# Normalising softmax probabilities on VectorE instead of GpSimd in a three-layer transformer kernel

## The chip, the cores and the metric

The program runs on one core of one Trainium2 chip. The metric is device time of one launch in microseconds. Times below are medians of executions on the chip; the profile is one execution of the same program, recorded instruction by instruction.

## What is computed

Two transformer blocks stand one after the other, on 512 tokens of width 1024, in float32. The first has two layers, the second one. Each layer is a mixer with several kinds of attention and a feed-forward part. The five softmax attentions are what the change touches:

```python
# layer 0: fox (8 heads, causal, forget gates) and chk (8 heads, chunks with a bias)
p = softmax(where(mask, q @ k.T * scale + bias, -inf));  o = p @ v
# layer 1: MLA (8 heads, chunk-causal); beside it 8 stick-breaking heads without a softmax
# layer 2: diff (4 heads)      a = softmax(s0) - lam * softmax(s1);  o = a @ v
#          NSA (8 heads)       o = g0 * o_cmp + g1 * (softmax(s_sel) @ v_sel) + g2 * (softmax(s_win) @ v_win)
```

All heads work on 512 queries by 512 keys. The rest are matrix products with the weights (projections, feed-forward), RMS norms, rotary embeddings and gates.

## The kernel before

**Tiling.** Activations lie transposed, 128 features by 512 tokens a tile. Weights stream from HBM in blocks of 128x1024 (`wblock`, L585). TensorE multiplies in a reduced form of float32, so every operand is kept as a high and a low part: ScalarE copies a block to its high part `wh`, VectorE subtracts to get the low part `wl`, and each product is three matmuls (`gemm`, L598). VectorE and ScalarE split activations in the same way.

**A softmax head.** `soft_head` (L820) does the four blocks of 128 queries of a head; block i has n = 128(i+1) keys. For each block `softmax` (L745) has two or three score matmuls into PSUM `pss`; then VectorE adds the mask and takes the row minimum in one custom instruction and reads its accumulator, ScalarE does the exponential with its row sum, VectorE the reciprocal of the sum, and GpSimd multiplies the block by the reciprocal (and in NSA by a gate column `gt`) in place. Then `turn` (L761) transposes on TensorE into PSUM `psp` and splits into `pt`, high part on ScalarE and low part on VectorE; `av` (L775) multiplies by the values into PSUM `pso`; `fold` (L782) adds the halves, `T<-pso,T` on VectorE, once a head. In diff heads every second block goes out unnormalised (`gate == "raw"`). The probability blocks are tiles `x`, their row statistics `sm`.

**The order of the work.** Nothing is issued directly. A recorder (L250) takes all instructions with what they read and write, and `schedule` (L391) places them: a list scheduler with a cost for each instruction (L322) and a latency between engines. On each engine it picks, of what is ready by its own clock, the instruction with the lowest priority number; attention comes first, and projections that are needed later (written under `later`) fill the gaps. In chk these fillers are the next heads' projections and half of the output projection; in NSA they are the products `ya`, `mg0` and `mg1` with their gates. Each engine then runs its queue in that order, and waits where a result isn't there yet. The cost of an instruction depends on its engine, so that a moved instruction shifts the order on all engines. All instructions are issued from L372, and so all rows of the profile have that line; the names of the tiles tell them apart. PSUM `psg` is what projections write.

```python
        if op.name == "tensor_scalar":            # GpSimd
            return 160 + 0.836 * n + 83 * k
        ...
            if op.name in ("memset", "tensor_copy") or (op.name == "tensor_scalar" and not psum):
                return 67 + 0.53 * n + 58 * k     # VectorE
```

Of the kernel before, what the change touches and what calls it, by code (L numbers as in the profile page):

```python
# [15 lines left out]
ALU = mybir.AluOpType  # L16
# [486 lines left out]
class Net:  # L503
# [241 lines left out]
    def softmax(self, i, passes, bias, gate=None):  # L745

        nc = self.nc
        n = 128 * (i + 1)
        s = self.scores(i, passes)
        p = self.tl("x", [128, 512])  # L750
        m = self.small(4)
        nc.vector.tensor_tensor_reduce(p[:, :n], s[:, :n], bias(i), scale=1.0, scalar=3e38,
                                       op0=ALU.add, op1=ALU.min, accum_out=m[:, 0:1])
        nc.scalar.activation(p[:, :n], p[:, :n], AF.Exp, scale=-1.0, bias=m[:, 0:1], accum_out=m[:, 1:2])
        nc.vector.reciprocal(m[:, 2:3], m[:, 1:2])
        if gate == "raw":
            return p, m[:, 2:3]
        nc.gpsimd.tensor_scalar(p[:, :n], p[:, :n], m[:, 2:3], 1.0 if gate is None else gate(i), ALU.mult, ALU.mult)
        return p

    def turn(self, ps_list):  # L761
# [1006 lines left out]
```

## Time and profile before

| | |
|---|---|
| median of three runs | 2076.8 us (2076.6 to 2078.18) |
| the profiled execution's own time | 2076.13 us |
| its span, first to last instruction | 2074.1 us |
| TensorE busy (weight loads beside it) | 97% (81%) |
| VectorE busy | 55% |
| ScalarE busy | 43% |
| GpSimd busy | 19% |
| mean granted TensorE clock | 0.993 of full speed |

The shares are means over the whole span. Attention takes some stretches of it, and in those VectorE and ScalarE are much busier than their means say; feed-forward stretches are TensorE's alone.

### The profile page before, as it was taken

How to read it: one execution, taken by the hardware profiler on the slowest of the kernel's cores; microseconds unless marked ns; L12 is line 12 of the kernel's file. 1: busy time of each engine (PE TensorE's matmuls, PEld its weight loads, DVE VectorE, ACT ScalarE, POOL GpSimd, SP SyncE). 2: the span in 40 equal slices, each digit the busy share in tenths (PEclk: the TensorE clock that was granted, in tenths of full speed). 3: DMA queues.
4: the chain of work that ended last, by engine and by line, in shares of the span. 5: the costliest groups of instructions: out<-in, count | busy, mean ns of one | idle time of the engine just before them, and what ended most of it. 6: DMA issues, size and time to landing. Idle time of an engine off the chain costs nothing. (4 is left out here: it accounts for less than half of the span.)

```text
span 2074.1 us, 27228 instructions
## 1 busy us (share of the span) xinstructions
PE 2017.1 (97%) x9958; PEld 1683.7 (81%) x9958; DVE 1131.8 (55%) x2033; ACT 895.1 (43%) x1621; POOL 396.5 (19%) x524
## 2 busy tenths in 40 slices
PE   8999999999999999999999999989999999999998
PEld 7888878888888877778888888867788888888887
DVE  5667853434445576774434344766786644333334
ACT  5556542322335555653323243543685543222224
POOL 2343210000022463220000014211340221011013
PEclk9999999999999999999999999999999999999999
DMA  6445623333344315632333334473213222223232
GB/s 199 129 129 154 198 83 100 94 99 97 97 139 127 102 62 131 180 115 92 102 93 101 94 122 135 122 182 116 71 42 112 92 101 92 101 93 102 91 102 82
DMA packets 80293, 231.98 MB, mean 112 GB/s; under 512 B 11424, under 2 KB 15392, under 8 KB 80160
## 3 DMA queue, kind: packets, MB, share of 16 engines
q1 hardware_dynamic: 80160, 230.25, 36.8%
q8 instruction: 78, 1.28, 0.3%
q14 instruction: 55, 0.45, 0.1%
HBM read 183.04 MB, written 10.49 MB: 93 GB/s over the span
## 5 line engine op out<-in xcount | busy, mean ns | idle before, releaser
L372 PE MATMUL psg<-h,wh 128*128 128x512 f32 x2688 | 848.4, 393 | 0.9 <-ACT h L372 0.6
L372 ACT ACTIVATE wh<-wr 128x1024 fp32r<-128x1024 f32 (+3 forms) x313 | 326.3, 1042 | 846.0 <-PE psg L372 672.9
L372 PEld LDWEIGHTS psg<-h,wh 128*128 128x128 f32 x2688 | 503.3, 189 | 102.0 <-ACT h L372 1.5
L372 PE MATMUL psg<-h,wl 128*128 128x512 f32 x1344 | 528.9, 393 | 1.2 <-DVE wl L372 1.0
L372 DVE TENSOR_TENSOR wl<-wr,wh 128x1024 fp32r<-128x1024 f32 (+3 forms) x313 | 384.7, 1229 | 59.9 <-ACT wh L372 58.7
L372 PEld LDWEIGHTS psg<-h,wl 128*128 128x128 f32 x1344 | 253.6, 189 | 53.9 <-DVE wl L372 3.1
L372 PE MATMUL psg<-KK,wh 128*128 128x512 f32 (+1 forms) x788 | 237.8, 383 | 0.4 <-DVE V L372 0.2
L372 DVE TENSOR_TENSOR x<-psg,x 128x512 f32<-128x512 f32 (+1 forms) x120 | 78.2, 654 | 281.8 <-PE psg L372 281.7
L372 POOL TENSOR_TENSOR acc<-acc,T 128x512 f32<-128x512 f32 (+1 forms) x50 | 72.9, 1457 | 775.7 <-issue 627.3
L372 PE MATMUL psg<-V,wh 128*128 128x512 f32 (+1 forms) x672 | 205.7, 387 | 1.1 <-DVE G L372 1.1
L372 PEld LDWEIGHTS psg<-KK,wh 128*128 128x128 f32 x788 | 146.3, 188 | 29.5 <-ACT o L372 0.6
L372 PE MATMUL psg<-KK,wl 128*128 128x512 f32 (+1 forms) x394 | 150.8, 383 | 0.0
L372 PEld LDWEIGHTS psg<-V,wh 128*128 128x128 f32 x672 | 125.6, 188 | 27.3 <-ACT wh L372 1.2
L372 DVE SCALAR_TENSOR_TENSOR T<-psg,rbc 128x512 f32<-128x512 f32 x64 | 44.2, 691 | 167.2 <-PE psg L372 166.8
L372 ACT ACTIVATE x<-x,sm 128x128 f32<-128x128 f32 (+1 forms) x192 | 106.6, 558 | 54.7 <-DVE sm L372 53.9
L372 PE MATMUL psg<-V,wl 128*128 128x512 f32 (+1 forms) x336 | 129.9, 387 | 0.0
L372 PE MATMUL psg<-o,wh 128*128 128x512 f32 x384 | 126.2, 397 | 0.8 <-ACT wh L372 0.5
L372 PE MATMUL psg<-wh,h 128*128 128x256 f32 (+2 forms) x560 | 114.5, 292 | 6.6 <-ACT wh L372 6.6
L372 PE MATMUL pso<-pt,V 128*128 128x128 f32 (+3 forms) x432 | 108.8, 340 | 3.4 <-ACT pt L372 1.9
L372 POOL TENSOR_SCALAR x<-x,sm 128x128 f32<-128x128 f32 (+1 forms) x112 | 65.9, 594 | 174.6 <-DVE sm L372 122.8
L372 PEld LDWEIGHTS psg<-wh,h 128*128 128x128 f32 x560 | 92.4, 194 | 8.4 <-ACT wh L372 6.6
L372 POOL TENSOR_TENSOR T<-T,rbc 128x512 f32<-128x512 f32 x22 | 39.2, 1782 | 280.5 <-ACT T L372 280.5
(263 smaller groups left out, 2667.6 us busy)
## 6 DMA issues: line engine op xcount, KB each, us to landing
wr<-in_w_dram SPq DMA_DIRECT2D x302, 512.0 KB, 3.5
KK<-AB SPq DMA_DIRECT2D x48, 256.0 KB, 5.4
QS<-AB SPq DMA_DIRECT2D x48, 128.0 KB, 4.0
x<-xs SPq DMA_DIRECT2D x24, 256.0 KB, 3.3
xs<-P SPq DMA_DIRECT2D x16, 256.0 KB, 3.9
xs<-x SPq DMA_DIRECT2D x16, 256.0 KB, 2.0
h<-AB SPq DMA_DIRECT2D x16, 256.0 KB, 4.1
KK<-AB SPq DMA_DIRECT2D x32, 128.0 KB, 2.3
```

The source lines that it names most:

```text
L372: op.inst = getattr(getattr(nc, op.eng), op.name)(*op.args, **op.kw)
```

## The change

The multiplication that normalises a block of probabilities goes to VectorE, behind the reciprocal that it needs. It stays in place, with the same operands. There are 176 of these: 32 in fox, 32 in chk, 32 in MLA, 16 in diff, 64 in NSA.

```diff
@@ def softmax(self, i, passes, bias, gate=None):
         nc.vector.reciprocal(m[:, 2:3], m[:, 1:2])
         if gate == "raw":
             return p, m[:, 2:3]
-        nc.gpsimd.tensor_scalar(p[:, :n], p[:, :n], m[:, 2:3], 1.0 if gate is None else gate(i), ALU.mult, ALU.mult)
+        nc.vector.tensor_scalar(p[:, :n], p[:, :n], m[:, 2:3], 1.0 if gate is None else gate(i), ALU.mult, ALU.mult)
         return p
```

The scheduler places everything anew. On VectorE, in NSA, after the score blocks of the last but one head. `ISA` with an x is the mask and minimum instruction, `ISA` with sm alone its accumulator read; pt is the low part of turned probabilities. Before:

```order
L372 TENSOR_TENSOR pt_2975_3047<-psp_3046,pt_2975_3047 128x256
L372 TENSOR_TENSOR pt_2977_3049<-psp_3048,pt_2977_3049 128x128
L372 SCALAR_TENSOR_TENSOR AB_2676<-AB_2676,G_2681 128x512
L372 RECIPROCAL sm_3077<-sm_3077 128x1
L372 ISA x_3082,sm_3083<-pss_3081,cst 128x512
L372 ISA sm_3083 128x1
L372 RECIPROCAL sm_3080<-sm_3080 128x1
L372 ISA x_3093,sm_3094<-pss_3092,cst 128x128
```

And after the change:

```order
L372 RECIPROCAL sm_3077<-sm_3077 128x1
L372 ISA x_3079,sm_3080<-pss_3078,cst 128x384
L372 ISA sm_3080 128x1
L372 TENSOR_SCALAR x_3073<-x_3073,sm_3074,gt_2434 128x128
L372 TENSOR_SCALAR x_3076<-x_3076,sm_3077,gt_2434 128x256
L372 TENSOR_TENSOR pt_2991_3063<-psp_3062,pt_2991_3063 128x512
L372 TENSOR_TENSOR pt_2993_3065<-psp_3064,pt_2993_3065 128x384
L372 RECIPROCAL sm_3080<-sm_3080 128x1
L372 ISA x_3082,sm_3083<-pss_3081,cst 128x512
L372 ISA sm_3083 128x1
L372 TENSOR_TENSOR pt_2995_3067<-psp_3066,pt_2995_3067 128x256
```

The normalisations stand in VectorE's queue among its other attention work, one or two rows behind their reciprocals, and the filler's row (AB, a gate) is gone from here.

On TensorE, in NSA, from the transposes of the last head's selected branch (psp, x the probabilities) into its product with the values (pso). psg with h and wh or wl are the filler's matmuls. Before:

```order
L372 MATMUL psp_3086<-cst,x_3082 128x128
L372 MATMUL psg_2686<-h_2191,wh_2688 128x512 x2
L372 MATMUL psg_2686<-h_2191,wl_2689 128x512
L372 MATMUL psg_2686<-h_2198,wh_2688 128x512 x2
L372 MATMUL pso_3071<-pt_3013_3085,V_2485 128x512
L372 MATMUL psg_2686<-h_2198,wl_2689 128x512
L372 MATMUL psp_3088<-cst,x_3079 128x128
L372 MATMUL psp_3088<-cst,x_3082 128x128
```

And after the change:

```order
L372 MATMUL pss_3101<-KK_2466,X_2557_2629 128x512 x2
L372 MATMUL psp_3084<-cst,x_3082 128x128
L372 MATMUL psp_3086<-cst,x_3082 128x128
L372 MATMUL pso_3071<-pt_3013_3085,V_2485 128x512
L372 MATMUL psp_3088<-cst,x_3079 128x128
L372 MATMUL psp_3088<-cst,x_3082 128x128
L372 MATMUL pso_3071<-pt_3013_3085,V_2485 128x512
L372 MATMUL pso_3071<-pt_3015_3087,V_2487 128x384
L372 MATMUL psp_3090<-cst,x_3082 128x128
```

Between transposes and product there were six filler matmuls, and now there is none; they come later in the queue.

On TensorE, in chk, the same place of the third head. Before, with the projection psg_592 between (its rows h_99 and h_101):

```order
L372 MATMUL psp_544<-cst,x_542 128x128
L372 MATMUL psp_546<-cst,x_536 128x128
L372 MATMUL psp_546<-cst,x_539 128x128
L372 MATMUL psp_546<-cst,x_542 128x128
L372 MATMUL psg_592<-h_99,wh_594 128x512 x2
L372 MATMUL psg_592<-h_99,wl_595 128x512
L372 MATMUL psg_592<-h_101,wh_594 128x512 x2
L372 MATMUL pso_552<-pt_473_545,V_438 128x512
```

And after the change:

```order
L372 MATMUL pss_564<-KK_522,QS_520 128x512 x2
L372 MATMUL psp_544<-cst,x_542 128x128
L372 MATMUL psp_546<-cst,x_542 128x128
L372 MATMUL pso_552<-pt_473_545,V_438 128x512
L372 MATMUL psp_548<-cst,x_539 128x128
L372 MATMUL psp_548<-cst,x_542 128x128
```

Here too the product with the values follows the transposes directly, and the projection comes behind the heads.

## Rows read from the trace of the kernel before

**Rows 1.** The page: busy time, share and instructions of each engine.

```profile
PE 2017.1 (97%) x9958; PEld 1683.7 (81%) x9958; DVE 1131.8 (55%) x2033; ACT 895.1 (43%) x1621; POOL 396.5 (19%) x524
```

**Rows 2.** Stretches (us): busy time (instructions) of each engine, PEclk, DMA share, GB/s.

```profile
core 0: us, PE busy (x) PEld busy (x) DVE busy (x) ACT busy (x) POOL busy (x), PEclk, DMA share, GB/s
320.00:360.00 40.00, 40.00 (x178) 33.13 (x177) 13.90 (x15) 7.44 (x7) 0.00 (x0) 1.00 0.32 94
163.93:189.62 25.69, 25.46 (x152) 21.69 (x151) 22.67 (x67) 20.52 (x54) 12.13 (x22) 1.00 0.44 124
825.49:840.99 15.50, 13.46 (x80) 11.90 (x81) 12.56 (x35) 11.95 (x31) 2.79 (x5) 0.89 0.44 122
1485.33:1574.75 89.42, 89.42 (x514) 74.89 (x513) 77.56 (x247) 70.81 (x189) 34.97 (x51) 1.00 0.19 63
189.62:213.89 24.27, 22.88 (x116) 18.70 (x115) 14.72 (x41) 12.39 (x29) 6.53 (x11) 1.00 0.71 194
```

**Rows 3.** Groups by operation: busy us, mean ns, idle of the engine before them, releasers.

```profile
L372 POOL TENSOR_SCALAR x<-x,sm 128x128 f32<-128x128 f32 (+1 forms) x112 | 65.9, 594 | 174.6 <-DVE sm L372 122.8 <-PE psg L372 33.9 <-PE psp L372 12.6
...
L372 POOL TENSOR_SCALAR x<-x,sm,gt 128x128 f32<-128x128 f32 (+1 forms) x64 | 44.0, 695 | 76.8 <-DVE sm L372 54.8 <-PE psp L372 12.5 <-PE psg L372 5.9
```

**Rows 4.** VectorE's tensor-scalar groups by shape, the same columns.

```profile
L372 DVE TENSOR_SCALAR strip<-strip,cst 128x512 f32<-128x512 f32 x2 | 1.0, 476 | 0.0
...
L372 DVE TENSOR_SCALAR P<-P 128x512 f32<-128x512 f32 x2 | 0.8, 421 | 0.0
...
L372 DVE TENSOR_SCALAR P<-P 62x256 f32<-62x256 f32 x2 | 0.6, 275 | 0.0
...
L372 DVE TENSOR_SCALAR gz<-gz 128x96 f32<-128x96 f32 x1 | 0.2, 195 | 0.0
```

**Rows 5.** VectorE in order of time, inside NSA: start us, us, instruction.

```profile
1503.42 0.15 DVE L372 RECIPROCAL sm<-sm 128x1 f32<-128x1 f32 x1
1503.49 0.27 DVE L372 CUSTOM_DVE_ANT_0 x<-pss,cst 128x128 f32<-128x128 f32 x1
1503.69 0.09 DVE L372 DVE_READ_ACCUMULATOR2_ANT sm<- 128x1 f32 x1
1503.69 0.42 DVE L372 CUSTOM_DVE_ANT_0 x<-pss,cst 128x256 f32<-128x256 f32 x1
```

**Rows 6.** VectorE's two-tensor form on the same blocks, diff heads, by shape.

```profile
L372 DVE SCALAR_TENSOR_TENSOR x<-x,sm,x 128x512 f32<-128x512 f32 x4 | 3.0, 745 | 0.2
L372 DVE SCALAR_TENSOR_TENSOR x<-x,sm,x 128x256 f32<-128x256 f32 x4 | 2.6, 658 | 0.0
L372 DVE SCALAR_TENSOR_TENSOR x<-x,sm,x 128x384 f32<-128x384 f32 x4 | 2.4, 610 | 0.0
L372 DVE SCALAR_TENSOR_TENSOR x<-x,sm,x 128x128 f32<-128x128 f32 x4 | 1.4, 348 | 0.0
```

**Rows 7.** GpSimd's groups from 1485.33 to 1574.75 us (NSA), all of them.

```profile
L372 POOL TENSOR_SCALAR x<-x,sm,gt 128x256 f32<-128x256 f32 (+3 forms) x51 | 35.0, 693 | 48.4 <-DVE sm L372 27.3 <-PE psp L372 12.5 <-PE psg L372 5.1
```

**Rows 8.** Later stretches, columns as in rows 2.

```profile
1574.75:1610.00 35.25, 35.25 (x157) 29.19 (x156) 19.39 (x25) 19.58 (x29) 0.00 (x0) 1.00 0.30 99
900.00:910.00 10.00, 9.72 (x43) 7.67 (x42) 9.96 (x13) 5.60 (x9) 4.62 (x3) 1.00 0.28 79
```

**Rows 9.** Who waited for whom: us in total, times, longest us; TensorE's rows.

```profile
PE psg L372 <- DMA rbcq<-in_w_dram: 5.5, 2, 5.1
...
PE psp L372 <- POOL x L372: 3.1, 5, 1.3
```

**Rows 10.** TensorE in order of time, MLA, at its longest wait for a normalisation.

```profile
834.72 0.44 PE L372 MATMUL psp<-cst,x 128*128 128x128 f32 x2 [1.26 <-POOL x L372]
```

**Rows 11.** VectorE and GpSimd in order of time, where a tensor-scalar meets GpSimd work.

```profile
908.97 0.92 DVE L372 TENSOR_SCALAR strip<-strip 128x512 f32<-128x512 f32 x1
...
908.07 1.53 POOL L372 TENSOR_TENSOR acc<-acc,T 128x512 f32<-128x512 f32 x1 [2.57 <-ACT T L372]
```

**Rows 12.** GpSimd's bias work in chk, from 163.93 to 189.62 us.

```profile
L372 POOL TENSOR_SCALAR strip<-strip 128x512 f32<-128x512 f32 x4 | 2.9, 723 | 0.5 <-DMA strip<-in_rel_dram 0.5
```

**Rows 13.** VectorE's other groups on which counts rest, NSA and chk stretches.

```profile
L372 DVE SCALAR_TENSOR_TENSOR AB<-AB,G 128x512 f32<-128x512 f32 x2 | 1.4, 688 | 0.1
...
L372 DVE TENSOR_TENSOR wl<-wr,wh 128x1024 fp32r<-128x1024 f32 x3 | 3.9, 1306 | 0.0
```

## The prediction

> **What bounds the kernel now.** I read the page first. TensorE is busy 97% of the span, VectorE 55%, GpSimd 19% [rows 1]. By those shares the change is free: VectorE has room, and GpSimd's normalisations, 112 in 65.9 us and 64 in 44.0 us [rows 3], leave an engine that TensorE rarely waits for. But shares are means over stages, so the next view is the busy time by stretch, cut where heads end (at the `T<-pso,T` of a head) [rows 2]. In feed-forward, 320 to 360 us, VectorE is busy 13.90 of 40 us. In the last seven of the eight NSA heads (1485.33 to 1574.75) it is busy 77.56 of 89.42 us, in the first four chk heads (163.93 to 189.62) 22.67 of 25.69, in three MLA heads (825.49 to 840.99) 12.56 of 15.50. In NSA TensorE never stops (89.42 of 89.42) only because filler matmuls stand between the steps of attention. There the question is whether VectorE can carry one instruction more per block.
>
> **The price of one normalisation on VectorE.** The trace has none of this form on VectorE, so I take it from the nearest rows, its tensor-scalars on float32 tiles [rows 4]. Without a column operand 96 elements last 195 ns and 512 last 421 ns: 226 ns for 416 elements, 0.54 ns each, and about 143 ns fixed (the row with 256 elements, 275 ns, fits: 282). One column operand makes 476 of 421, so 55 ns a column. With one column the four sizes last 267, 337, 407 and 476 ns, with two (NSA has the gate) 322, 392, 462 and 531. Back to back an instruction starts some 0.08 us before the one ahead has ended (1503.42 + 0.15 against 1503.49) [rows 5], so a place in the queue costs 0.08 less: 0.29 us on average with one column, 0.35 with two. From below the one-column price bounds it, 0.29. From above the two-tensor form on the same blocks does, 348 to 745 ns, mean 590 [rows 6], 0.51 a place. I take 0.35, the end that the tensor-scalar rows are nearest to. The Trainium skill's page VectorE: DVE Perf Modes (Mode 2×_2P) says that an instruction with one tensor source, all in SBUF, handles two float32 elements a cycle; the 0.54 ns agree for one column. No row has two columns; by the page a column is not a second tensor and 0.35 holds, without the mode it would be the upper end, and the sum below some 12 us larger.
>
> **NSA.** The stretch has 51 normalisations [rows 7], 12 of 128 keys and 13 of each other size by the order: 21.9 us less 51 x 0.08, 17.8 us. The order also takes three filler evacuations of 0.69 us [rows 13] out of this stretch of VectorE's queue and brings two score instructions in, about 1.0 us less. VectorE's work becomes 77.6 + 17.8 - 1.0 = 94.4 us. TensorE's queue between the same two points loses filler: counted over the orders, 149 matmuls of 512 columns stood there, and now 105. A filler matmul takes 40.00/178 = 0.225 us [rows 2], so 44 are 9.9 us, which are still to be done behind the heads; there TensorE is full already [rows 8], so nothing hides them. What is left for TensorE here is about 89.4 - 9.9 = 79.5 us, against 94.4 on VectorE: VectorE becomes the bound of NSA. Rows show it up to 9.96 of 10 us busy [rows 8]; with 98% the stretch takes 94.4/0.98 = 96.3 us. The loss is 96.3 + 9.9 - 89.4 = **16.8 us**.
>
> **chk.** The same sum for its first four heads: 15 normalisations with one column (three of the smallest size), 4.5 us; one weight split (1.31 us [rows 13]) and two projection evacuations fewer, one more of the values, together -2.0 us: 22.67 + 4.5 - 2.0 = 25.2 us, at 98% 25.7. TensorE loses 27 + 13 + 1 filler matmuls and keeps 10 + 4: 27 x 0.225 = 6.1 us go behind the heads. 25.7 + 6.1 - 25.69 = 6.1 us. In the next stretch TensorE idles 24.27 - 22.88 = 1.39 us now [rows 2], which the later filler can cover. Loss **4.7 us**.
>
> The Trainium skill's page SBUF — State Buffer (Who interferes with whom) has a rule against the change: a VectorE instruction in the two-port mode and a GpSimd instruction lock each other out. One row agrees: a tensor-scalar that met GpSimd work lasted 0.92 us, alone 0.42 [rows 11, 4]. In NSA GpSimd has nothing left to collide with [rows 7]; in chk the four bias preparations remain [rows 12], and by the rule they could add 4 x 0.5 = 2 us, a sum of 2098. I take none of it.
>
> **MLA.** In the three heads from 825 us 7 normalisations (2.2 us), one score instruction, two reciprocals and a weight split more, an evacuation less (together 1.0 us): 12.56 + 3.2 = 15.7 us, at 98% 16.0 instead of 15.50; TensorE's own part there grows by some 0.2 us of scores. Loss **0.7 us** allowing for that. The next three MLA heads, fox and diff have VectorE room; I cost them at nothing, and say below what it costs if that cover is gone.
>
> **What is gained.** The hop to GpSimd and back goes. TensorE waited for normalisations 5 times, 3.1 us in all [rows 9]. The longest, 1.26 us, is in the MLA heads already counted [rows 10]; the rest, **1.8 us**, is won. GpSimd's 109.9 us are nobody's bound. A further TensorE wait, 5.1 us for a weight tile of the compression [rows 9], hangs on SyncE's queue, where eight copies of keys stand ahead of its load, and these wait for a low-part split on VectorE; the new order has that split some rows earlier. It can shrink to nothing, or grow, since TensorE also gets there with less filler. I take no change and keep 5.1 us as a bound.
>
> **Sum.** 16.8 + 4.7 + 0.7 - 1.8 = 20.4 us on the profiled execution's 2076.13 us, which stands within 0.7 us of the median of 2076.8: **2096 us**.
>
> **The rivals.**
>
> *VectorE has room after all: faster.* Its busy time would have to contain waiting that shrinks when others wait. The change then only shortens each head's chain, and gives 2076.1 - 3.1 - 5.1 = 2068 us. For it speaks the 12 us in which VectorE idles in NSA. The point that decides: VectorE's work in NSA must stay under TensorE's 79.5 us, so a normalisation may cost (79.5 - 77.6 + 1.0)/51 = 0.06 us. The cheapest row is five times that. Chance 0.07.
>
> *Losses and gains cancel: no change.* VectorE runs without a hole, at the one-column price (NSA 91.4 us, loss 11.9; chk 25.2, loss 4.2), and the 1.8 and 5.1 us are won: 2085 us. For less still, filler would have to find holes behind the heads, which the rows do not show. Chance to end within 0.2% of before, 0.08.
>
> *Dearer than I take it.* At the upper price 0.51 NSA gains another 51 x 0.16 = 8.3 us and chk 15 x 0.22 = 3.3: 2108 us. The same comes of queues that wait for each other: attention is a chain through four engines, and with no filler between its steps VectorE may be busy only 90% of chk and 92% of NSA (28.0 and 102.6 us, 8.6 us more together, 2105), as chk's 22.67 of 25.69 today would suggest. That is also what it costs if the cover in fox or diff is gone. Chance 0.15.
>
> *The change doesn't do what it says.* The order shows 176 tensor-scalars on VectorE and none of them on GpSimd; that is excluded.
>
> **How the numbers follow.** The forecast, VectorE-bound NSA and chk with a loss of 10 to 27 us, has 0.70. The range goes from 2084 (no hole, cheap price, the weight wait gone) to 2109 (dear price or holes, not both in full) and leaves out the faster rival and most of the unchanged one. A measurement of this kernel can tell 0.2%, some 4 us, from no change. Faster by more than that 0.07, within it 0.08, slower 0.85.
>
> **What would show it.** In the profile after, GpSimd has 176 instructions less; VectorE's tensor-scalars on x last 0.27 to 0.53 us; between the same two NSA heads VectorE is busy over 95% and TensorE under 85%, with waits of transposes and value products for VectorE (x, pt); and the span grows by about those waits. I am wrong if TensorE is still full in NSA, if the price is outside 0.29 to 0.51 us a place, or if the time is lost elsewhere, in fox, diff or around the compression's weights.

## The result, and the profile after

| | before | after |
|---|---|---|
| median of four runs each, taken together | 2077.49 us (2076.6 to 2086.22) | 2115.14 us (2113.63 to 2117.79) |
| ratio, 95% interval | | 1.0171 (1.0148 to 1.0194) |
| the profiled execution's own time, span | 2076.13, 2074.1 us | 2113.65, 2111.9 us |
| mean granted TensorE clock | 0.993 | 0.987 |

The change costs some 36 us (31 to 40), 1.7%. The prediction had the sign; its 2096 us is 19 us short, and the result lies outside its range. The page's busy line, which answers to [rows 1]:

```profile
PE 2038.9 (97%) x9958; PEld 1689.0 (80%) x9958; DVE 1190.7 (56%) x2209; ACT 897.8 (43%) x1621; POOL 286.4 (14%) x348
```

GpSimd has 176 instructions less and VectorE 176 more, as many as were moved. VectorE is busy 58.9 us longer, 0.335 us a normalisation. TensorE's share hardly moves and says nothing of the loss. The stretches after, with the columns of [rows 2]: the first four chk heads and what follows, three MLA heads, diff with the compression and the first NSA head, the last seven NSA heads, and behind them:

```profile
161.17:188.42 27.25, 23.27 (x126) 18.20 (x126) 24.81 (x80) 19.53 (x52) 3.61 (x8) 0.94 0.24 75
188.42:218.07 29.65, 28.94 (x144) 23.96 (x143) 19.22 (x52) 14.01 (x31) 2.52 (x4) 1.00 0.63 180
829.27:846.62 17.35, 15.14 (x82) 12.02 (x82) 15.38 (x45) 11.90 (x33) 0.00 (x0) 0.90 0.37 97
1302.00:1507.36 205.36, 189.41 (x981) 149.10 (x979) 139.50 (x366) 86.85 (x197) 18.50 (x15) 0.94 0.45 125
1507.36:1603.78 96.42, 90.28 (x488) 70.40 (x487) 92.88 (x300) 70.20 (x188) 0.00 (x0) 1.00 0.15 50
1603.78:1640.00 36.22, 36.22 (x161) 29.98 (x161) 19.58 (x26) 18.61 (x28) 0.00 (x0) 1.00 0.30 102
```

The fourth of these was not shown of the profile before; it begins at the same value projection and ends with the first NSA head:

```profile
1291.80:1485.33 193.53, 181.21 (x988) 146.04 (x987) 130.73 (x342) 88.28 (x201) 35.71 (x43) 0.99 0.48 132
```

The stretches begin and end at the same work (the cut ahead of diff only to 0.3 us: by the value eviction there, at 1291.77 and 1302.31 us, the 4.6 and 11.8 us below are 4.9 and 11.5). So their ends tell how late the program is at each place. The differences to the profile before are the account of the 37.8 us of span, of one execution of each kernel:

| to | before, us | after, us | late by | gained or lost on the way | predicted |
|---|---|---|---|---|---|
| end of fox, start of chk's four heads | 163.93 | 161.17 | -2.8 | -2.8 | part of -1.8 |
| end of these four heads | 189.62 | 188.42 | -1.2 | +1.6 | |
| end of the next stretch | 213.89 | 218.07 | +4.2 | +5.4 (chk +7.0) | +4.7 |
| start of three MLA heads | 825.49 | 829.27 | +3.8 | -0.4 | 0 |
| their end | 840.99 | 846.62 | +5.6 | +1.8 | +0.7 |
| the projection ahead of diff's end | 1291.80 | 1302.00 | +10.2 | +4.6 | 0 |
| end of the first NSA head | 1485.33 | 1507.36 | +22.0 | **+11.8** | 0 |
| end of the last NSA head | 1574.75 | 1603.78 | +29.0 | +7.0 | |
| the end | 2074.1 | 2111.9 | +37.8 | +8.8 (NSA +15.8) | +16.8 |

NSA came out within 1 us of its term. The largest miss is diff with the first NSA head, which I had costed at nothing. The row to the three MLA heads hides two things: chk's last head ends at 248.62 instead of 241.68 us, 6.9 us late, so that its last three heads lost 2.7 us more, and by 829.27 us 3.2 us of the lateness are gone again. TensorE's waits after, as in [rows 9]:

```profile
PE psp L372 <- DVE x L372: 7.7, 5, 3.2
...
PE psg L372 <- DVE wl L372: 5.3, 10, 1.3
PE pss L372 <- DVE sm L372: 4.9, 10, 1.1
...
PE psg L372 <- DMA rbcq<-in_w_dram: 1.0, 1, 1.0
```

The waits for normalisations on GpSimd, 3.1 us in all, are gone, and waits of transposes for VectorE, 7.7 us, stand in their place. The longest is at the end of diff; VectorE and then TensorE in order of time there:

```profile
1424.29 1.21 DVE L372 TENSOR_TENSOR wl<-wr,wh 128x1024 fp32r<-128x1024 f32 x1
1425.42 0.21 DVE L372 RECIPROCAL sm<-sm 128x1 f32<-128x1 f32 x2
1425.55 0.46 DVE L372 SCALAR_TENSOR_TENSOR V<-psg,rcol,V 128x256 fp32r<-128x256 f32 x1
1425.93 0.47 DVE L372 TENSOR_SCALAR x<-x,sm 128x512 f32<-128x512 f32 x1
1426.33 0.15 DVE L372 TENSOR_TENSOR sm<-sm,lam 128x1 f32<-128x1 f32 x1
1426.40 0.34 DVE L372 COPY P<-psg 128x62 f32<-128x62 f32 x2
1426.66 0.74 DVE L372 SCALAR_TENSOR_TENSOR x<-x,sm,x 128x512 f32<-128x512 f32 x1
```

```profile
1423.89 0.33 PE L372 MATMUL psg<-cst,P 62*128 62x62 f32 x2
1427.45 0.69 PE L372 MATMUL psp<-cst,x 128*128 128x128 f32 x2 [3.23 <-DVE x L372]
```

A weight split, a value eviction and a copy stand in VectorE's queue around the last diff head's reciprocal, normalisation and combination, and the next entry of TensorE's queue has to wait for them. The same wait, 3.2 us, is there when GpSimd normalises in the same order (the second experiment below):

```profile
PE psp L372 <- DVE x L372: 3.7, 2, 3.2
```

So it belongs to the order, not to the instruction.

### The profile page after: what moved, and what is told of

Read it like the earlier page. It is cut to its first block, busy times and chain, and to the rows that moved or that the text cites. A ratio compares the mean times of both kernels' runs of the same rounds, so it can differ in the third digit from the quotient of the medians.

```text
span 2111.9 us, 26861 instructions
## 1 busy us (share of the span) xinstructions
PE 2038.9 (97%) x9958; PEld 1689.0 (80%) x9958; DVE 1190.7 (56%) x2209; ACT 897.8 (43%) x1621; POOL 286.4 (14%) x348
## 5 line engine op out<-in xcount | busy, mean ns | idle before, releaser
L372 ACT ACTIVATE x<-x,sm 128x128 f32<-128x128 f32 (+1 forms) x192 | 106.8, 558 | 57.6 <-DVE sm L372 57.0
L372 PE MATMUL psp<-cst,x 128*128 128x128 f32 x440 | 90.9, 285 | 11.2 <-DVE x L372 7.7
L372 PEld LDWEIGHTS psg<-wh,h 128*128 128x128 f32 x560 | 91.4, 192 | 11.5 <-ACT wh L372 6.9
L372 ACT ACTIVATE pt<-psp 128x512 fp32r<-128x512 f32 (+3 forms) x176 | 70.5, 435 | 62.2 <-PE psp L372 59.4
```

The source lines that it names most:

```text
L372: op.inst = getattr(getattr(nc, op.eng), op.name)(*op.args, **op.kw)
```

## The experiments

Medians of all runs, each compared with the kernel before on the same chip. The medians of before were 2076.1 to 2079.6; all its runs lie between 2069.5 and 2089.9, so that under some 4 us only a ratio's interval speaks. "NSA" below is the stretch of the last seven heads, before 89.42, after 96.42 us.

**Order and engine apart.** The scheduler plans the normalisation for one engine and another executes it. First the order of before, executed by VectorE:

```diff
-        nc.vector.tensor_scalar(p[:, :n], ...)
+        op = nc.gpsimd.tensor_scalar(p[:, :n], ...)
+        op.run = "vector"
...
-        op.inst = getattr(getattr(nc, op.eng), op.name)(*op.args, **op.kw)
+        op.inst = getattr(getattr(nc, op.run), op.name)(*op.args, **op.kw)
```

> The order of before on every engine (the scheduler still plans the normalisation as GpSimd work), but VectorE executes it, at the place in time where GpSimd's instruction stood. Theory A (VectorE's added work is the loss, the new order only spreads it): in the last seven NSA heads VectorE has 77.6 + 51 x 0.37 = about 96 us of work, so the stretch takes 97 to 100 us instead of 89.4, chk some 28 instead of 25.7; no filler has moved behind the heads, so NSA and chk lose 10 to 13 us; with what diff and MLA lose, 2088 to 2098. Theory B (the new order is the loss, VectorE would have carried the work): within 4 us of before, 2073 to 2081, and TensorE full in NSA.

Measured: 2095.96 us, ratio 1.0093 (1.0056 to 1.0130), some 19 us slower. In the profiled execution, 21.5 us late at the end of the last NSA head, 7.7 us are NSA's last seven heads, 4.3 chk's eight, and 3.8 lie between the last MLA head and the end of the first NSA head. Another 4.2 us lie between chk's last head and 681.69 us, where nothing is normalised and the granted clock was 0.57 from 656 to 664 us: part of this execution's loss isn't the normalisations'. And the order of the change, executed by GpSimd (the two names exchanged):

> The order of the changed kernel (the scheduler plans the normalisation as VectorE work), but GpSimd executes it. Theory A: VectorE has its old work, about 77 us in the seven NSA heads against 79.5 us that TensorE has left there, so the heads take 80 to 88 us, with 9.9 us of filler behind them: a loss of 0 to 8 us in NSA, little in chk and diff; 2076 to 2090. Theory B: the order makes the loss, 2105 to 2116, and the waits of diff and NSA are there as in the changed kernel.

Measured: 2109.77 us, ratio 1.0162 (1.0140 to 1.0184), 34 us slower. Nearly the whole loss is there although VectorE has none of the new work. NSA in the two, columns as in [rows 2], the first executed by VectorE, the second by GpSimd:

```profile
1499.14:1596.25 97.11, 94.90 (x514) 74.42 (x513) 93.51 (x298) 71.72 (x189) 0.00 (x0) 1.00 0.18 58
```

```profile
1504.71:1600.80 96.09, 89.62 (x488) 69.96 (x487) 78.35 (x249) 70.10 (x188) 35.29 (x51) 1.00 0.15 50
```

With the order kept, VectorE is busy 96% and sets NSA's 97.11 us, as expected for a full VectorE, but no filler moves. In the new order NSA takes 96 us too, with VectorE busy only 82%. So in this stretch either cause suffices alone, and the two don't add: it has two limits that lie close together.

**The load taken away.** VectorE normalises the first column of a block alone, in the order of before and in the new one:

```diff
+        op.args = (p[:, :1], p[:, :1], *op.args[2:])
```

> The order of before, with VectorE executing the normalisation, but of the first column of each block alone (the other columns stay unnormalised, which is left out of the computation). The instruction stands at the same place of VectorE's queue and the first transposes of a block wait for it, but it costs VectorE about 0.1 us a place instead of 0.35. Theory A (VectorE's load decides in this order: the whole instruction made NSA's last seven heads 97.1 us instead of 89.4): VectorE is then busy some 83 us there, under TensorE's 89, and the stretch goes back to 88 to 91 us; total 2074 to 2083. Theory B (the place decides: the normalisation waits behind other work of an in-order queue, whatever it lasts): the stretch stays at 94 to 97 us and the total at 2087 to 2097.

Measured: 2078.06 us, ratio 0.9998 (0.9978 to 1.0017): the whole loss is gone.

> The order of the changed kernel, VectorE normalises the first column of each block alone (the rest is left out). Theory A (VectorE is the bound of NSA after the change): with some 14 us less VectorE work the last seven NSA heads fall from 96.4 to 80 to 86 us, and the total to 2085 to 2100. Theory B (the new order keeps TensorE waiting for the chain between the engines, because filler no longer stands between its steps; VectorE's load is second): NSA stays at 90 to 96 us, diff and the first NSA head still lose 8 us or more against before, and the total stays at 2100 to 2113.

Measured: 2105.87 us, ratio 1.0139 (1.0106 to 1.0173): the loss stays. NSA in the two, old order first:

```profile
1486.82:1577.73 90.91, 90.85 (x515) 74.91 (x514) 85.07 (x299) 71.32 (x189) 0.00 (x0) 1.00 0.19 61
```

```profile
1503.90:1598.69 94.79, 89.19 (x487) 70.32 (x487) 85.66 (x299) 69.85 (x188) 0.00 (x0) 1.00 0.15 51
```

VectorE is busy alike in both. In the old order its load was the cause; in the new one the order is.

**One part at a time.** The engine is chosen by the kind of head, and the scheduler plans accordingly:

```diff
+        e = nc.vector if part in ("nsa",) else nc.gpsimd
-        nc.vector.tensor_scalar(p[:, :n], ...)
+        e.tensor_scalar(p[:, :n], ...)
```

> The normalisation goes to VectorE in the NSA heads alone (64 of 176). Theory A: the last seven heads cost 16 us as in the changed kernel (stretch 96 us, 9.9 us of filler behind), the first head some us more: 2093 to 2101, and until 1400 us the times of before. If instead the loss around the first NSA head and the compression (the changed kernel is 10.5 us late at 1286 us and 24.2 late at the first NSA head's end) comes of the diff heads' own normalisations, this kernel is at most 2 us late there.

> The normalisation goes to VectorE in the diff heads alone (16 of 176). Theory A1 (the loss in diff comes of waits for VectorE that let TensorE's granted clock fall to 1.2 GHz again and again; the changed kernel has 23.8 us at that level between 1403 and 1492 us, before has 3.4): 8 to 14 us late behind the first NSA head, 2085 to 2091, with low clock for over 10 us there. Theory A2 (the diff stretch loses by the NSA normalisations in the first head): 2075 to 2080.

> Only the 32 normalisations of chk go to VectorE. Theory (the reordered chk heads lose filler that TensorE then does behind them, and each head's chain has no cover): the first four heads take 27 to 28 us instead of 25.7, the last chk head ends 8 to 11 us late, and of it 6 to 10 us stay to the end: 2081 to 2088. Rival (what chk loses is given back at the waits for transfers behind it): 2075 to 2080.

> Only the 32 normalisations of MLA go to VectorE. Theory (the same as in chk, on a smaller scale: 23 projection matmuls between the steps of three heads become 16): the MLA heads end 3 to 5 us late and the total is 2078.5 to 2082. Rival (MLA's chain is not the bound and the hop to GpSimd is won): 2073 to 2077.

> Only the 32 normalisations of fox go to VectorE, the other 144 stay on GpSimd. Theory A (fox has VectorE room, and the hop to GpSimd and back goes): fox ends 2 to 3 us earlier, as it did in the changed kernel, and the total is 2072 to 2076. Rival (the gain is given back at the next wait for a transfer, the keys of chk or the accumulator behind it): within 1 us of before, 2075.5 to 2078.

| only | median, us | ratio | interval |
|---|---|---|---|
| NSA | 2094.88 | 1.0095 | 1.0068 to 1.0122 |
| diff | 2089.43 | 1.0061 | 1.0040 to 1.0083 |
| chk | 2086.15 | 1.0031 | 1.0012 to 1.0051 |
| MLA | 2080.34 | 1.0010 | 0.9991 to 1.0028 |
| fox | 2077.20 | 0.9999 | 0.9983 to 1.0016 |

NSA's stretch took 96.46 us again. The ratios add to 41 us, the whole change has 36, with some 4 us of uncertainty in each. Fox ended 3.5 us earlier, in the changed kernel 2.8, and the total shows nothing of it, though its interval reaches 3.5 us below no change. MLA lost less than can be told from no change. Then diff alone undone (`part in ("fox", "chk", "mla", "nsa")`):

> The changed kernel with one part undone: the 16 normalisations of diff stay on GpSimd, so that diff has the order of before; fox, chk, MLA and NSA are as changed. Theory (diff's new order costs by itself, by waits of transposes for VectorE and the low TensorE clock behind them): the 9 to 13 us come back and the total is 2100 to 2107. Rival (diff only shows what the first NSA head and the compression would lose anyway): under 5 us come back, 2109 to 2116.

Measured: 2101.97 us, ratio 1.0105 (1.0076 to 1.0134), 13 us below the change, what diff alone costs. The stretch of diff in this kernel, and in the one with diff alone:

```profile
1300.70:1492.09 191.39, 179.46 (x974) 145.77 (x973) 133.29 (x350) 86.55 (x196) 27.70 (x30) 0.98 0.48 133
```

```profile
1294.50:1498.12 203.62, 189.68 (x987) 149.06 (x986) 136.63 (x358) 88.41 (x201) 26.23 (x27) 0.96 0.45 126
```

VectorE has some 3 us more in 12 us more time, and is busy 67% of it: it isn't full in diff. What the stretch loses stands in two places. Against the profile before (193.53 us, TensorE busy 181.21) the one with diff alone has 1.6 us more in which TensorE idles and 8.5 us more in which it is busy, with as many matmuls at a lower clock (0.96 for 0.99); the changed kernel has 3.6 and 8.2 (0.94). The waits that the profile shows are the smaller part; how far the clock makes the larger is bounded in the last section.

**Is diff's loss one of its order?** Diff alone again, with 60 or 110 ns more reckoned for each normalisation, which changes the order only:

```diff
+        op.cost += 60 if op.eng == "vector" else 0
```

> Only diff's 16 normalisations on VectorE, and the scheduler reckons 60 ns more for each. Around the last diff head TensorE's queue then has 9 and 14 filler matmuls of 280 columns between the pairs of transposes, where the order made without the 60 ns has 34 ahead of all of them and 7 behind, and before had 11, 20 and 8. Theory (the loss in diff hangs on where this filler stands: with 34 of them spent early TensorE waits 3.2 us for VectorE and then runs at the low clock): that wait is under 1.5 us and the total 2074 to 2083. Rival (it hangs on VectorE's work or on other waits in diff): 2086 to 2092, as when diff alone was moved.

> Only diff's 16 normalisations on VectorE, and the scheduler reckons 110 ns more for each, near what they last in the trace. Around the last diff head 31 filler matmuls stand ahead of the transposes, then 14, then 2. Theory (the loss hangs on where this filler stands): 7 filler matmuls more between the last two pairs of transposes shorten the wait by about 1 us only, 2084 to 2091. Rival (a truer cost mends the order): 2075 to 2083.

Measured: 2082.68 us, ratio 1.0022 (1.0003 to 1.0041), and 2078.80, ratio 0.9999 (0.9984 to 1.0015). With the same work on the same engine the loss of 13 us is gone with 110 ns, and all but some 5 us of it with 60, so it is the order's. But it didn't hang on the filler around the last head as I expected: that stood better with 60 ns, and 110 ns did better. There the longest wait of a transpose for x is 0.9 us, where I had expected 2.2. Diff's stretch with 110 ns:

```profile
1292.40:1485.89 193.49, 183.19 (x984) 145.84 (x984) 135.82 (x358) 88.35 (x201) 26.20 (x27) 0.98 0.47 132
```

VectorE is as busy as in the slow one (135.82 and 136.63 us), in 10 us less. The 110 ns also bring the reckoned price near the measured one; so the whole change with them, and with 100 ns more from VectorE and ScalarE to TensorE instead:

```diff
+        op.cost += 110
```

> The changed kernel, all 176 normalisations on VectorE, with 110 ns more reckoned for each by the scheduler, near what they last in the trace. With this cost diff alone lost nothing. 44 projection matmuls stay in the first four chk heads (changed 37, before 64), 101 in the last seven NSA heads (105, 149). Theory (diff's loss is an accident of one order and goes away, chk's and NSA's is filler taken out of attention and stays): the first NSA head ends 8 to 13 us less late than in the changed kernel, NSA's last seven heads take 95 to 97 us, and the total is 2099 to 2108. Rival (the scheduler's too low price made the whole loss): NSA's stretch with what moves behind it loses under 10 us, total 2080 to 2096.

```diff
-        "vector": dict(tensor=245, ...
-        "scalar": dict(tensor=275, ...
+        "vector": dict(tensor=345, ...
+        "scalar": dict(tensor=375, ...
```

> The changed kernel, all 176 normalisations on VectorE, but the scheduler reckons 100 ns more from VectorE and from ScalarE to TensorE, so that it puts filler between the steps of attention again: 63 projection matmuls in the first four chk heads (before 64, changed 37) and 122 in the last seven NSA heads (149 and 105). Theory B (missing filler between the steps is what costs): chk loses under 4 us instead of 8 to 9, the first NSA head no longer adds 6, and the total is 2086 to 2101. Theory A (VectorE's load alone decides in chk and NSA): NSA takes 96 us or more with 6 us of filler still moved behind it, chk is as late as in the changed kernel, and the total stays at 2106 to 2116.

Measured: 2111.15 us, ratio 1.0160 (1.0127 to 1.0192), above both expectations, and 2105.46, ratio 1.0139 (1.0112 to 1.0166), between them. With the truer price diff and the first NSA head take some 9 us less than in the changed kernel, the MLA heads lose 6 us more, and NSA stays at 96.6 us: it mends one place and spoils another. With the longer latency NSA takes 96.53 us and 6.1 us are lost behind it, as theory A had it. In chk theory B comes nearer: the first four heads, with their filler back in (152 matmuls recorded, as before), take longer, but less is left to do behind them, so that chk has lost 3.2 us instead of 7.0 by the end of the next stretch and 6.8 instead of 9.7 by its last head:

```profile
160.94:190.25 29.31, 27.42 (x152) 21.53 (x151) 27.67 (x83) 21.16 (x53) 3.80 (x8) 1.00 0.34 105
```

**Does any new order cost?** GpSimd normalises and is planned, with 100 ns less or more reckoned for it (`op.cost -= 100`, `op.cost += 100`):

> The kernel before with all its work on its engines (GpSimd normalises), but the scheduler reckons 100 ns less for each normalisation, so that all orders are made anew: 62 projection matmuls stay in the first four chk heads (before 64), 125 in the last seven NSA heads (149). Theory B1 (a new order costs by the filler that it takes out of attention, whichever engine normalises): chk and diff as before within 3 us, NSA and what follows 3 to 6 us late by 24 matmuls of 0.225 us; total 2079 to 2086. Theory B2 (the order of before is a lucky one, any other costs): total 2088 to 2110. Rival (only orders made for VectorE cost): 2074 to 2080.

> The same with 100 ns more for each normalisation on GpSimd: 64 projection matmuls in the first four chk heads as before, 134 in the last seven NSA heads (before 149), the last diff head as before. Theory B1 (loss by filler taken out of attention): 15 x 0.225 = 3.4 us late behind NSA at most, total 2077 to 2084. Theory B2 (any other order costs): 2088 to 2110. Rival (only orders made for VectorE cost): 2074 to 2080.

Measured: 2084.50 us, ratio 1.0033 (1.0015 to 1.0050), and 2084.32, ratio 1.0021 (1.0005 to 1.0038). These two departures from the order of before cost 4 to 7 us without moving any work; the order made for VectorE costs 34. NSA of the first of these:

```profile
1489.60:1576.02 86.42, 86.20 (x497) 71.62 (x496) 76.38 (x244) 69.14 (x188) 33.86 (x50) 1.00 0.20 62
```

**What the new order lacks.** One more order, executed by GpSimd: made as for VectorE, but whoever needs the normalised block waits 1.5 us more.

```diff
+            if op.run != op.eng:
+                end += 1500
```

> GpSimd executes all 176 normalisations. The order is made as for VectorE, but the scheduler lets whoever needs a normalised block wait 1.5 us more. Then between the last score matmul of a block and its first transposing matmul TensorE's queue has 47 matmuls in NSA (median; before 54, changed 37) and 50 in the first four chk heads (55, 33), while the filler in these stretches is no more than in the changed order: 78 projection matmuls in the last seven NSA heads (149, 105) and 39 in chk (64, 37). The order of the changed kernel run by GpSimd took 96.1 us in NSA and 27.2 in chk. Theory L (what the new order lacks is the distance between scores and transposes, which hides the chain): NSA 80 to 88 us, chk 21 to 25. Rival (the filler itself is lacking, or GpSimd's time in the chain sets the pace): NSA 92 to 97, chk 26 to 28. The total hangs on what moves behind the heads too: 2080 to 2095 by L, 2100 to 2115 by the rival.

Measured: 2118.47 us, ratio 1.0188 (1.0167 to 1.0209), no faster than the change itself (the intervals overlap). The first four chk heads took 25.98 us, at the rival's edge. NSA:

```profile
1511.65:1601.02 89.37, 83.21 (x459) 64.53 (x459) 74.30 (x243) 64.58 (x180) 32.70 (x51) 1.00 0.15 48
```

89.37 us lies between the two expectations, and a sum tells why. Take from NSA's stretch the filler that the trace has in it (`psg` matmuls), at the 0.225 us a matmul of [rows 2]; what is left is what attention took for itself, with the waits (the trace has 365 to 374 other matmuls in each). The counts in the expectations above are of the queue from value product to value product; the stretch runs to the fold on VectorE behind them, and up to 12 more filler matmuls fall into it.

| kernel | executed by | filler | matmuls, scores to transposes | NSA, us | less the filler |
|---|---|---|---|---|---|
| before | GpSimd | 149 | 54 | 89.42 | 55.9 |
| before, 100 ns less reckoned | GpSimd | 128 | 55 | 86.42 | 57.6 |
| before, 100 ns more reckoned | GpSimd | 138 | 56 | 88.61 | 57.6 |
| order of before, one column | VectorE | 150 | 54 | 90.91 | 57.2 |
| order of before | VectorE | 149 | 54 | 97.11 | 63.6 |
| the change | VectorE | 117 | 37 | 96.42 | 70.1 |
| its order, one column | VectorE | 117 | 37 | 94.79 | 68.5 |
| its order | GpSimd | 117 | 37 | 96.09 | 69.8 |
| the change, 100 ns more latency | VectorE | 127 | 38 | 96.53 | 68.0 |
| the change, 110 ns more reckoned | VectorE | 105 | 35 | 96.61 | 73.0 |
| the order with 1.5 us more | GpSimd | 87 | 47 | 89.37 | 69.8 |

Orders planned for GpSimd leave 56 to 58 us, with VectorE's full load 64; orders planned for VectorE leave 68 to 73, whoever executes. In those, filler taken out or put in only moves time, and more distance between scores and transposes alone doesn't mend it. What would is not settled; filler and distance were never given back together.

Nor do the waits on record single out the normalised blocks. After the change TensorE idles 6.1 us in NSA, of which 0.4 us ended with such a block; the low parts of the turned probabilities and a weight split ended more:

```profile
L372 PE MATMUL psp<-cst,x 128*128 128x128 f32 x133 | 26.2, 283 | 2.0 <-DVE pt L372 1.5 <-DVE x L372 0.4
L372 PE MATMUL psg<-h,wl 128*128 128x512 f32 x24 | 9.9, 414 | 1.5 <-DVE wl L372 1.5
```

**A version for where VectorE has room.** The order of before, with VectorE executing fox, MLA and diff only:

```diff
+        op.run = "vector" if self.part in ("fox", "mla", "diff") and gate is None else "gpsimd"
```

> The order of before on all engines, and VectorE executes the 80 normalisations of fox, MLA and diff, where it has room; chk and NSA stay on GpSimd. Theory (with the order kept and VectorE not full, only the hop to GpSimd and back goes): 1 to 4 us faster than before, 2072 to 2076. Rival (the hop is hidden behind other work there too, and what fox wins is given back at the next wait for a transfer): no difference, within 1 us of before.

Measured: 2080.17 us, ratio 1.0006 (0.9988 to 1.0023): no difference. A gain of over 2.5 us is excluded: the hop to GpSimd was hidden, or what it won was given back. No kernel here was shown to beat the one before.

## Why the prediction was wrong in size

**The price of a normalisation held, in the main.** 0.29 and 0.35 us a place make 54.9 us for 112 and 64; VectorE's busy time grew by 58.9. By shape in NSA's last seven heads after, with two columns:

```profile
L372 DVE TENSOR_SCALAR x<-x,sm,gt 128x512 f32<-128x512 f32 x13 | 7.0, 541 | 0.0
L372 DVE TENSOR_SCALAR x<-x,sm,gt 128x384 f32<-128x384 f32 x13 | 6.2, 474 | 0.0
L372 DVE TENSOR_SCALAR x<-x,sm,gt 128x256 f32<-128x256 f32 x13 | 5.3, 406 | 0.0
L372 DVE TENSOR_SCALAR x<-x,sm,gt 128x128 f32<-128x128 f32 x12 | 4.1, 342 | 0.0
```

I had 531, 462, 392 and 322 ns. The upper end, 0.51, is out. Between 128 and 512 elements a further one costs 0.52 ns. In the first four chk heads, with one column, 128, 256 and 384 elements lasted 277, 346 and 410 ns, so that the second column adds 60 to 65 ns, where I had 55. Over the whole kernel the small one-column blocks are dearer than the 267 and 337 ns that I had, and the last section says why:

```profile
L372 DVE TENSOR_SCALAR x<-x,sm 128x256 f32<-128x256 f32 x28 | 11.3, 404 | 0.3
L372 DVE TENSOR_SCALAR x<-x,sm 128x128 f32<-128x128 f32 x28 | 9.8, 350 | 0.3
```

The rule that I weighed (the Trainium skill, VectorE: DVE Perf Modes, section Mode 2×_2P) is that an instruction with one tensor source handles two float32 elements a cycle. The trace agrees for two columns as well: 0.52 ns an element, as against 0.54 without a column.

**NSA: the term was right (16.8 forecast, 15.8 measured), its reason half right.** VectorE is busy 96% and the stretch takes 96.42 us, where I had 96.3. But I said that TensorE would need about 79.5 us there and that VectorE alone would be the bound, and took TensorE under 85% busy as its sign; it was busy 94%. With VectorE's load taken away the stretch still took 94.8 to 96.1 us. The 79.5 us came from subtracting 44 filler matmuls from a stretch in which TensorE showed no wait. By the trace only 32 left the stretch (149 to 117), and the new order itself holds TensorE up to about the length that VectorE's load would; neither was in the sum, and why the order does so is open. That two limits came out alike made the term right: that is luck.

**chk: mis-sized.** 4.7 us forecast, 7.0 measured by the same two stretches. The four heads took 27.25 us where I had 25.7, VectorE busy 91% of it instead of 98%: the holes that I had put into a rival. The last three chk heads, 2.7 us, were in no term.

**MLA: mis-sized,** 0.7 against 1.8 us; alone it can't be told from no change.

**The gain of 1.8 us did not come.** The waits that it was to remove went, and waits for VectorE of 7.7 us took their place. Fox ended 2.8 us early; alone, its gain couldn't be seen in the total.

**The failed step is the sentence "The next three MLA heads, fox and diff have VectorE room; I cost them at nothing".** VectorE has that room in diff (busy 68% after), and the stretch with the first NSA head still lost 11.8 us; with diff's 16 left on GpSimd 13 us came back. Room in a share of busy time says nothing of when an instruction stands in the queue: the reordered queue put, for one, a weight split and an eviction ahead of the last head's chain. With another order the same load cost nothing. Of a further 4.6 us between the three MLA heads and diff 1.3 came in the other MLA heads (889.14 to 896.04 us at their end), and 2.9 in a stretch at low clock behind them (last section). The sum worked out load and filler; a loss by the order itself was in no term.

**The rivals.** "Dearer", with its queues that wait for each other, 2105 us and a chance of 0.15, named the right kind of mechanism, but I bounded it by a VectorE busy 90 to 92%, and it went on through diff. Its remark that the same would be lost if the cover in diff were gone was right in size, but the sum left it out, and the range with it. The faster rival and the one of no change are refuted. The last of my signs of being wrong, time lost in fox, diff or around the compression, is the one that came true. Two sums of the prediction are a little off: its total is 2096.5 us, and the rival of no change, with MLA's 0.7 us, 2086; no bound of the range hangs on either.

**The weight wait of the compression** fell from 5.5 to 1.0 us; I had left it unchanged with 5.1 us as a bound. It can't be booked as a gain: with fox alone on VectorE, where this part was not moved, it was 1.3 us. It varies between runs.

## What to carry to other kernels

Where a scheduler makes the order, moving one instruction is two changes, work and order. Plan for one engine and execute on the other, both ways, before explaining anything by load: here the order alone cost 34 us, the load alone 19, both 36. The 19 us are the least certain of these, with an interval of 12 to 27. A new order brings waits of its own: in diff they came where load and filler foretold no loss, so an engine's free share doesn't make a stretch safe. A reordering that moves no work is the control: here two of them cost 4 to 7 us.

## What the runs showed that I had not expected

**The clock takes part.** In the stretch of diff the granted clock falls to half (1.2 of 2.4 GHz) four times after the change, once before. The four after, and the one before:

```profile
1403.10:1409.90 6.80, 5.84 (x18) 3.09 (x17) 1.05 (x3) 1.72 (x4) 0.49 (x1) 0.50 0.53 179
...
1427.00:1433.80 6.80, 6.35 (x16) 3.08 (x17) 4.03 (x8) 1.36 (x3) 0.00 (x0) 0.50 0.50 173
1471.40:1478.20 6.80, 5.44 (x16) 4.20 (x17) 5.63 (x14) 2.15 (x5) 0.98 (x1) 0.50 0.23 60
1488.50:1491.90 3.40, 3.40 (x12) 2.70 (x12) 1.20 (x6) 1.39 (x6) 0.00 (x0) 0.51 0.52 167
```

```profile
1399.00:1402.40 3.40, 2.95 (x7) 1.66 (x8) 0.00 (x0) 0.00 (x0) 0.00 (x0) 0.50 0.04 16
```

Four matmuls of the compression last 1.94 us in the first of these, and 1.08 us at full clock:

```profile
1404.55 1.94 PE L372 MATMUL psg<-rbcq,strip 128*62 128x256 f32 x4 [0.96 <-DMA rbcq<-in_w_dram]
...
1411.71 1.08 PE L372 MATMUL psg<-rbcq,strip 128*62 128x256 f32 x4
```

TensorE was busy 21.0 us in the four and 2.95 us in the one; half of the difference, 9 us, is my estimate of the most that the clock cost here. TensorE's busy time in the stretch grew by 8.2 us. Each fall follows waits of TensorE, of 0.9 to 1.4 us ahead of the first, 3.2, 1.8 and 2.2 us ahead of the others, and 5.1 us ahead of the one before. But not every wait brings it. In the same place, behind the wait for the accumulator, TensorE ran on at full clock before and at half for 6.9 us after:

```profile
914.69 1.05 PE L372 MATMUL pss<-cst,acc 128*128 128x1 f32 x8 [1.72 <-POOL acc L372]
```

```profile
922.28 1.86 PE L372 MATMUL pss<-cst,acc 128*128 128x1 f32 x8 [1.67 <-POOL acc L372]
```

After the change two waits of 0.6 us stood shortly ahead of it. All four kernels with the wait of 3.0 to 3.2 us in diff have a fall behind it, so what the wait and what the clock cost can't be parted here.

**A busy TensorE hides waiting.** NSA's stretch has 26 matmuls less after by the trace (488 instead of 514), some 6 us at 0.225; TensorE is yet busy 90.28 instead of 89.42 us, at full clock in both. Matmul ends are modelled, as the profile's legend says, so part of the waiting seems to be counted as work. "TensorE never stops" in [rows 2] was no proof that nothing waits.

**A normalisation can be held up by GpSimd.** A normalisation of 256 elements with one column lasted 346 ns in chk; this one met GpSimd:

```profile
1381.34 1.29 POOL L372 TENSOR_TENSOR G<-G,G 128x512 f32<-128x512 f32 x1 [1.65 <-DVE sm L372]
1381.37 1.42 DVE L372 TENSOR_SCALAR x<-x,sm 128x256 f32<-128x256 f32 x1
```

It lasts as long as GpSimd's instruction and ends behind it. The rule that I named and put at 2 us in chk (the Trainium skill, SBUF — State Buffer, section Who interferes with whom) is that a VectorE instruction in the two-port mode and a GpSimd instruction lock each other out. The trace agrees for VectorE, locked out here for some 1.1 us; GpSimd's instruction lasted 1.29 us, as most of its kind do. It reaches few: three normalisations lasted over 0.8 us beside GpSimd work, and in fox five of 128 elements lasted 0.67 instead of 0.28 us, each beside GpSimd's work on a bias strip:

```profile
45.94 0.67 DVE L372 TENSOR_SCALAR x<-x,sm 128x128 f32<-128x128 f32 x1
```

That is some 5 us of VectorE's time in all, and makes the small blocks' means larger than forecast. I had looked for it in chk; most of it came in fox, which ended early all the same.
